# Three quarters of the up projection as pairs of panels, seven block products a pair

## The chip, the cores and the metric

One core of a Trainium2 chip. The time of a kernel is its device time in microseconds, the median of its runs. The engines are TensorE (PE; weight loads are listed apart as PEld), VectorE (DVE), ScalarE (ACT), GpSimd (POOL) and SyncE (SP, which here only issues DMAs).

## The reference

One layer of a decoder trunk in float32: 512 prompt tokens and 8 single-token samples share the weights. Both attentions end in `mix` and `h`; what the change touches is the feed-forward, whose product with `w_up` (1024 x 4096) is followed by a squared relu.

```python
mix = jax.nn.sigmoid(ga) * (oa @ w_pa) + jax.nn.sigmoid(gb) * (ob @ w_pb)
h = x + mix @ w_o
f = jnp.square(jax.nn.relu(rmsnorm(h, g_norm2) @ w_up))
return h + f @ w_down
# D_MODEL = 1024, D_FF = 4096; then y = rmsnorm(h + f @ w_down, g_final)
```

The outputs are also the caches moved on by a token, 42 MB of them plain copies from input to output.

## The kernel before

Activations lie transposed: 128 partitions, 8 tiles of the inner dimension (`k`), 520 columns (512 prompt and 8 sample tokens, in two halves `HC` of 260). A product of float32 is made in fp32r: weights and activations are each split into a high and a low part, and three matmuls are added up: high x high, high weight x low activation, low weight x high activation (`passes`). ScalarE makes the high part (`whi`, L86), VectorE the low one (`wlo`, L87), in pieces of 4 inner tiles (128x512).

The weights come in panels of 128 output columns, in the order of the list `order` in `run()`: the input projection, `w_pa`, `w_pb`, `w_o` (8 panels), then four quarters `qd` of the feed-forward, each of 8 panels of `w_up` and 8 of `w_down`; the last eight `w_down` panels (`lw`) run in column groups at the end (L1212). `panel_mms` loads panel i+2 on SP's queue, splits panel i+1, and issues the 48 matmuls of panel i (`k_tile`, L137), each 128x128 weights by 128x260. Four buffers hold split weights (`wbufs`).

After each `w_o` panel VectorE adds it to the residual `H`, and ScalarE and VectorE make `hh` and `hl`, the two parts of `H` times the norm's weight; the squares are summed in `acc`. Behind the first `w_up` panel two matmuls over `ones` (into `r2`) sum `acc` over the partitions; `rv` becomes the mean square and then its reciprocal (L1171). The feed-forward is homogeneous, so `rv` is first used in the last quarter. Each `w_up` panel is followed by ScalarE's relu from PSUM, VectorE's square and the two parts `fh` and `fl`; each `w_down` panel by an add into `dd` on VectorE. After each panel `pace()` puts one 1 MiB copy of a cache on POOL's DMA queue, which starts when the panel's last matmul is done, until the 42 copies are out.

A scheduler, fed with estimated durations, sets the order of the instructions on each engine; each engine then runs its own in that order. `tc.high_priority()` lets what is inside go ahead of what is ready, and `behind(x, y)` keeps two instructions in order.

Of the kernel before, what the change touches and what calls it, by code (L numbers as in the profile page):

```python
# [45 lines left out]
class Build:  # L46
    def __init__(self, ctx, tc, I, O):
# [32 lines left out]
    def raw_tile(self, i):  # L80
        return self.rawp.tile([P, self.panels[i][1], P], F32, tag="raw", name="raw", bufs=self.rawb)

    def split_piece(self, raw, x, n, dst=None):
        nc = self.nc
        hi, lo = dst or (self.wp.tile([P, n, P], F32R, tag=t, name=t, bufs=self.wbufs) for t in ("whi", "wlo"))
# [883 lines left out]

    def run(self):  # L970
# [146 lines left out]
        nc.vector.tensor_tensor(oal, self.oa, oah.bitcast(F32), op=ALU.subtract)  # L1117
        obh, obl = self.big("obh", F32R), self.big("obl", F32R)
        self.split_big(self.R, obh, obl)
        with pool("late") as p:  # L1120
            for x in range(2):
                for k, ps in enumerate(self.panel_mms(oah, oal, 4), 4 * x):
                    ga = halves(gA[:, k])
                    for o, i in ((ga[:, 0], ps[0]), (ga[:, 1], ps[1])) if isinstance(ps, list) else ((ga, ps),):
                        nc.vector.tensor_tensor(o, i, o, op=ALU.mult)
# [26 lines left out]
            self.rawp, self.rawb = p, 3  # L1152
            fh, fl = self.big("fh", F32R), self.big("fl", F32R)
            dd = self.big("dd")
            for qd in range(4):
# [4 lines left out]
                for k in range(KT):  # L1160
                    if qd == 3 and k == KT - 1:
# [3 lines left out]
                    if qd == 0 and k == 0:  # L1165
                        for j in range(2):
                            pr = self.bank("r2")
                            nc.tensor.matmul(pr[:, :HC], self.ones, acc[:, j * HC:(j + 1) * HC], start=True, stop=True)
                            nc.vector.tensor_scalar(rv[:, j * HC:(j + 1) * HC], pr[:, :HC], 1 / D, EPS,
                                                    op0=ALU.mult, op1=ALU.add)  # L1170
# [226 lines left out]
```

## Time and profile before

| | |
| --- | --- |
| median of 3 runs | 910.67 us (910.57 to 910.96) |
| span of the profiled execution, first to last instruction | 909.0 us |
| busy: PE, PEld | 898.3 (99%), 881.4 (97%) |
| busy: DVE, ACT, POOL | 548.6 (60%), 368.2 (41%), 72.3 (8%) |
| mean granted clock of TensorE | 0.996 |
| moved by DMA | 155.72 MB, mean 171 GB/s |

The profiled execution's own time is its span; the median of the runs, which hold no profile, lies 1.7 us above it. A group's row gives the source line, engine, operation, what is written and read, the shape and count; then the busy time and the mean of one in ns; then the idle time of that engine just before these instructions and what ended it. The chain of waits follows the instruction that ended last back to what released each step. A row of time stretches gives the busy time and count for each engine, the granted clock, the share of the DMA engines and GB/s.

### The profile page before, as it was taken

What the parts mean: (1) busy time and instruction counts of PE and PEld (TensorE: products, weight loads), DVE (VectorE), ACT (ScalarE), POOL (GpSimd) and SP (SyncE); (2) the same over time, 40 slices, a digit from 0 to 9 for tenths busy, and PEclk for the clock granted to TensorE, in tenths of its full rate; (3) what the DMA queues carried; (4) which work ended last, traced back from release to release, by engine and by line L of the source; (5) the groups of instructions that cost most, each with busy time, mean ns of one, the idle gap of its engine ahead of it and who ended that gap; (6) DMA issues with size and microseconds to landing.
All of it is one profiled execution on the core that took longest, in us unless ns stands there. A gap on an engine that the chain in (4) does not pass through costs nothing.

```text
span 909.0 us, 19543 instructions
## 1 busy us (share of the span) xinstructions
PE 898.3 (99%) x8154; PEld 881.4 (97%) x8154; DVE 548.6 (60%) x1083; ACT 368.2 (41%) x732; POOL 72.3 (8%) x127
## 2 busy tenths in 40 slices
PE   9999999999999999999999999999999999999996
PEld 8999999999999999999999999999999999999995
DVE  6867666865957769586655564433443345556643
ACT  6234324453645454456333444323432243224432
POOL 1110000000111212010000000000000000000000
PEclk9999999999999999999999999999999999999998
DMA  7476365324634632221688787777772222223302
GB/s 252 142 247 217 118 211 209 118 71 144 211 109 155 234 125 103 88 72 53 227 320 289 277 301 278 279 274 282 267 276 107 94 93 94 93 94 116 117 14 82
DMA packets 37728, 155.72 MB, mean 171 GB/s; under 512 B 5308, under 2 KB 10436, under 8 KB 35816
## 3 DMA queue, kind: packets, MB, share of 16 engines
q1 hardware_dynamic: 32248, 94.79, 29.8%
q0 software_dynamic: 5104, 59.20, 18.2%
q8 instruction: 64, 1.05, 0.5%
q10 hardware_dynamic: 288, 0.49, 0.1%
q14 instruction: 24, 0.20, 0.1%
HBM read 140.73 MB, written 54.17 MB: 214 GB/s over the span
## 4 chain that ended last, share of the span: by engine, by line
PE 98%; DMA 1%; DVE 0%; ACT 0%; SPq 0%; DVEq 0%; issue 0%; ACTq 0%
PE mps L137 83%; PE mps L1212 5%; PE mps L298 1%; PE lev L727 1%; PE sps L473 1%; PE pvp L506 1%; PE gpo L836 1%; PE gpu L840 1%; PE ptp L490 1%; PE vps L437 1%; PE gpo L838 1%; DMA xr<-in_xT 1%; PE gso L908 0%; PE gop L860 0%; PE gsp L925 0%; PE gps L668 0%
## 5 line engine op out<-in xcount | busy, mean ns | idle before, releaser
L86 ACT ACTIVATE whi<-raw 128x512 fp32r<-128x512 f32 (+1 forms) x266 | 165.0, 624 | 367.5 <-PE mps L137 339.0
L87 DVE TENSOR_TENSOR wlo<-raw,whi 128x512 fp32r<-128x512 f32 (+1 forms) x266 | 180.5, 681 | 130.0 <-ACT whi L86 128.8
L137 PE MATMUL mps<-uh,whi 128*128 128x260 f32 x896 | 255.9, 286 | 0.0
L137 PE MATMUL mps<-ul,whi 128*128 128x260 f32 x896 | 255.8, 286 | 0.0
L137 PE MATMUL mps<-uh,wlo 128*128 128x260 f32 x896 | 255.3, 285 | 0.0
L137 PEld LDWEIGHTS mps<-uh,wlo 128*128 128x128 f32 x896 | 168.8, 188 | 2.1 <-issue 1.5
L137 PEld LDWEIGHTS mps<-ul,whi 128*128 128x128 f32 x896 | 168.8, 188 | 1.2 <-issue 0.3
L137 PEld LDWEIGHTS mps<-uh,whi 128*128 128x128 f32 x896 | 168.8, 188 | 1.1 <-issue 0.7
L137 PE MATMUL mps<-hh,whi 128*128 128x260 f32 x512 | 144.8, 283 | 0.0
L137 PE MATMUL mps<-hh,wlo 128*128 128x260 f32 x512 | 144.8, 283 | 0.0
L137 PE MATMUL mps<-hl,whi 128*128 128x260 f32 x512 | 144.2, 282 | 0.0
L137 PE MATMUL mps<-fh,whi 128*128 128x260 f32 x384 | 108.2, 283 | 0.0
L137 PE MATMUL mps<-fh,wlo 128*128 128x260 f32 x384 | 108.1, 283 | 0.0
L137 PE MATMUL mps<-fl,whi 128*128 128x260 f32 x384 | 107.7, 282 | 0.0
L137 PEld LDWEIGHTS mps<-hh,whi 128*128 128x128 f32 x512 | 96.4, 188 | 0.0
L137 PEld LDWEIGHTS mps<-hh,wlo 128*128 128x128 f32 x512 | 96.3, 188 | 0.0
L137 PEld LDWEIGHTS mps<-hl,whi 128*128 128x128 f32 x512 | 96.3, 188 | 0.0
L137 PEld LDWEIGHTS mps<-fh,whi 128*128 128x128 f32 x384 | 72.3, 188 | 0.0
L137 PEld LDWEIGHTS mps<-fh,wlo 128*128 128x128 f32 x384 | 72.1, 188 | 0.0
L137 PEld LDWEIGHTS mps<-fl,whi 128*128 128x128 f32 x384 | 72.1, 188 | 0.0
L1212 PE MATMUL mps<-fh,lw 128*128 128x280 f32 (+1 forms) x256 | 46.8, 284 | 0.0
L1212 PEld LDWEIGHTS mps<-fh,lw 128*128 128x128 f32 x256 | 39.7, 189 | 0.1
(343 smaller groups left out, 1388.5 us busy)
## 6 DMA issues: line engine op xcount, KB each, us to landing
raw<-in_w_in SPq DMA_DIRECT2D x55, 512.0 KB, 4.3
raw<-in_w_up SPq DMA_DIRECT2D x32, 512.0 KB, 4.2
raw<-in_w_down SPq DMA_DIRECT2D x32, 512.0 KB, 4.3
sx<-in_state SPq DMA_DIRECT2D x8, 512.0 KB, 4.2
sx<-dV SPq DMA_DIRECT2D x8, 512.0 KB, 4.8
out_sgla<-sx POOLq DMA_DIRECT2D x8, 512.0 KB, 5.4
raw<-in_w_pb SPq DMA_DIRECT2D x8, 512.0 KB, 3.3
raw<-in_w_o SPq DMA_DIRECT2D x8, 512.0 KB, 7.1
```

What stands on the lines that cost most here:

```text
L86: self.piece = (nc.scalar.activation(hi, raw[:, x:x + n], AF.Copy), nc.vector.tensor_tensor(lo, raw[:, x:x + n], hi.bitcast(F32), op=ALU.s ...
L87: nc.vector.tensor_tensor(lo, raw[:, x:x + n], hi.bitcast(F32), op=ALU.subtract))
L137: self.last = self.nc.tensor.matmul(o[:, :HC], wt, x[:, k, j * HC:(j + 1) * HC], start=(k == 0 and n == 0), stop=(k == kt - 1 and n == 2))
L298: self.last = nc.tensor.matmul(ps[i][:, j, :HC], wt, u[:, k, j * HC:(j + 1) * HC], start=(k == 0 and n == 0), stop=(k == KT - 1 and n == 1))
L437: nc.tensor.transpose(pt[:, r * P:(r + 1) * P], vt[:, r * P:(r + 1) * P], self.c["ident"])
L473: m = nc.tensor.matmul(pss[hh][:, hp, c], Q[rows, i, b * P:(b + 1) * P], K[rows, i, ks], start=True, stop=True)
L490: nc.tensor.transpose(pt[:, hh, x], prs[hp][:, hh, x * P:(x + 1) * P], self.c["ident"])
L506: m = nc.tensor.matmul(po[64 * hh:64 * hh + 64, hp * P:(hp + 1) * P], v, pTs[hp][:, hh, x], start=(x == first), stop=(x == 1))
L727: m = self.nc.tensor.matmul(out, w, x, start=True, stop=True)
L836: nc.tensor.matmul(po[:, :256], ST[:, c], V[:, c], start=True, stop=(c == 0))
L838: nc.tensor.matmul(po[:, :256], qe[:, c * P:(c + 1) * P], st, start=False, stop=True)
L1212: nc.tensor.matmul(ps, w, u[:, kk, cc], start=(kk == 0 and x == 0), stop=(kk == KT - 1 and x == 2))
```

## The change

In quarters 0 to 2 (the prediction's quarters 1 to 3) two `w_up` panels are one entry of `order`, marked `PAIR`. Let the first panel's inner tiles 0 to 3 be A11 and 4 to 7 be A12, the second's A21 and A22, and B11, B12, B21, B22 the blocks of the activations (`hh`, `hl`), the first index the half of the inner tiles and the second the half of the columns. The second panel's results come out with the sign turned, so that its weights' sums need no subtraction. Each product is 4 inner tiles x 3 passes = 12 matmuls:

| product | weights | activations |
| --- | --- | --- |
| P1 | A11 | B11 |
| P5 | A21+A22 | B11-B12 |
| P2 | A12 | B21 |
| P6 | A11+A21+A22 (`s2`) | -(B11-B12+B22) |
| P3 | A11+A12+A21+A22 (`s4`) | B22 |
| P7 | A11+A21 | B22-B12 |
| P4 | A22 | B11-B12+B22-B21 |

PSUM adds P2 to P1, P3 to P5 and P7 to P6. The first panel's halves are P1+P2 and (P1+P6)+(P5+P3), the second's, with the sign turned, (P1+P6+P7)+P4 and (P1+P6+P7)+P5. VectorE's P1+P6 is the prediction's v6. P1 and P5 are copied from PSUM by ScalarE for these adds.

The weights' sums come in three ways: `sums` is loaded with the second panel (A21, A22), and a DMA of POOL's queue that adds to what is there (`accum_op=ALU.add`, 512 KB) turns it into A11+A21 and A21+A22; POOL makes `s2` and `s4` from it with two adds; `ra` (the first panel) and `rb` (A22) are plain loads. That is 7 split pieces a pair where two panels had 4. The sums of activations, T with the parts `Th` and `Tl`, are made tile by tile behind each `w_o` panel (`column_sums`) from a float32 copy `hg` of what `hh` and `hl` are split from. `AHEAD` is how many pieces the code splits ahead of the product in hand; `first_pairs` are the pairs that open a quarter: they run P2 before P6, the others P6 before P2. A fifth buffer of split weights and a third of raw panels lie in the pool `late`. Constants that the feed-forward does not use move to the pool `mid`, closed before it, and the feed-forward's work tiles share the name `t`. `pace()` is called once a pair instead of once a panel.

```diff
+    def load_pair(self, i):
+        ap, p = self.panels[i][0], self.late
+        sums = p.tile([P, KT, P], F32, tag="sums", name="sums", bufs=2)
+        self.load(sums, ap[1])
+        self.nc.gpsimd.dma_start(sums.rearrange("p (i k) n -> p i (k n)", i=2),
+                                 ap[:, :, :4].rearrange("i p k n -> p i (k n)"), accum_op=ALU.add)
+        ra = self.raw_tile(KT)
+        self.load(ra, ap[0])
+        rb = p.tile([P, 4, P], F32, tag="rb", name="rb", bufs=2)
+        self.load(rb, ap[1][:, 4:])
...
+    def pair_pieces(self, i):
...
+        yield self.split_piece(ra, 0, 4)
+        yield self.split_piece(sums, 4, 4)
+        s2, s4 = new(), new()
+        nc.gpsimd.tensor_tensor(s2, sums[:, 4:], ra[:, :4], op=ALU.add)
+        nc.gpsimd.tensor_tensor(s4, s2, ra[:, 4:], op=ALU.add)
...
+    def pair_mm(self, acts, done):
...
+        mid = (("P2", a, False), ("P6", b, True)) if i in self.first_pairs else (("P6", b, True), ("P2", a, False))
+        prev = None
+        for q, (n, o, fresh) in enumerate((("P1", a, True), ("P5", c, True), *mid, ("P3", c, False), ("P7", b, False),
+                                           ("P4", a, True))):
+            with self.tc.high_priority():
+                self.pieces_to(i, q + AHEAD)
+            if q == 4 and i + 2 < len(self.panels):
+                self.load_panel(i + 2)
+            hi, lo = self.ready[i][q]
+            for k in range(4):
+                xh, xl = acts(n, k)
+                for x, (w, u) in enumerate(((hi, xh), (hi, xl), (lo, xh))):
...
+                    if prev is not None:
+                        self.behind(mm, prev)
...
+    def column_sums(self, p, b, k, hi, lo):
...
+            e = nc.vector if k == KT - 1 else nc.gpsimd
+            e.tensor_tensor(t[:, 0], b22, b12, op=ALU.subtract)
+            nc.vector.scalar_tensor_tensor(t[:, 1], t[:, 0], -1.0, b11, op0=ALU.mult, op1=ALU.subtract)
+            nc.vector.scalar_tensor_tensor(t[:, 2], t[:, 1], -1.0, b21, op0=ALU.mult, op1=ALU.subtract)
...
+        nc.scalar.activation(hi[:, x, ts], t, AF.Copy)
+        nc.vector.tensor_tensor(lo[:, x, ts], t, hi[:, x, ts].bitcast(F32), op=ALU.subtract)
...
+    def up_pair(self, p, work, k, fh, fl):
...
+        def split(x):
+            nc.scalar.activation(t[x], t[x], AF.Square)
+            nc.scalar.activation(fh[:, k + x], t[x], AF.Copy)
+            nc.vector.tensor_tensor(fl[:, k + x], t[x], fh[:, k + x].bitcast(F32), op=ALU.subtract)
...
+            if n in ("P1", "P5"):
+                v[n] = new(n)
+                with tc.high_priority():
+                    nc.scalar.activation(v[n], o, AF.Copy)
+            elif n == "P2":
+                nc.scalar.activation(t[0][:, one], o, AF.Relu)
+            elif n == "P6":
+                v[n] = new(n)
+                with tc.high_priority():
+                    nc.vector.tensor_tensor(v[n], v["P1"], o, op=ALU.add)
+            elif n == "P3":
+                nc.vector.tensor_tensor(t[0][:, two], v["P6"], o, op=ALU.add)
+                nc.scalar.activation(t[0][:, two], t[0][:, two], AF.Relu)
+                split(0)
+            elif n == "P7":
+                v[n] = new(n)
+                nc.vector.tensor_tensor(v[n], v["P1"], o, op=ALU.add)
+                nc.vector.tensor_tensor(t[1][:, two], v[n], v["P5"], op=ALU.add)
+            else:
+                nc.vector.tensor_tensor(t[1][:, one], v["P7"], o, op=ALU.add)
+                nc.scalar.activation(t[1], t[1], AF.Relu, scale=-1.0)
+                split(1)
+                self.pace(1)
...
-            order += [(I["w_up"][qd * 8 + i], KT) for i in range(8)]
+            if qd < 3:
+                self.first_pairs.add(len(order))
+                order += [(I["w_up"][qd * 8 + i:qd * 8 + i + 2], PAIR) for i in range(0, 8, 2)]
...
+                nc.scalar.activation(hg[:, k], H[:, k], AF.Copy, scale=self.g("n2", k))
+                nc.vector.tensor_tensor(hl[:, k], hg[:, k], hh[:, k].bitcast(F32), op=ALU.subtract)
+                self.column_sums(p, hg, k, Th, Tl)
...
+                if qd < 3:
+                    for k in range(0, KT, 2):
+                        self.pair_mm(acts, self.up_pair(p, work, k, fh, fl))
+                        if qd == 0 and k == 0:
+                            spread()
```

What this does to the order shows at three places. On VectorE, where the first `w_up` panel ends and the reciprocal stands, before (`L87` is a low part of weights, `L1178` and `L1180` the first panels' square and low part):

```order
L1169 TENSOR_SCALAR rv<-r_7061 128x260
L87 TENSOR_TENSOR wlo<-raw,whi 128x512
L1169 TENSOR_SCALAR rv<-r_7064 128x260
L1178 SCALAR_TENSOR_TENSOR fsq<-mps,relu 128x520
L1171 RECIPROCAL rv<-rv 128x520
L1180 TENSOR_TENSOR fl<-fsq,fh 128x520
L87 TENSOR_TENSOR wlo<-raw,whi 128x512 x2
L1178 SCALAR_TENSOR_TENSOR fsq<-mps,relu 128x520
```

And the same place of the changed kernel (`L1072` is the last of the last tile's three T sums, `L1075` T's low part, `L108` a low part of weights, `L1098` v6, `L1100` the add for P3):

```order
L1072 SCALAR_TENSOR_TENSOR tr<-tr,hg 128x260
L1318 TENSOR_SCALAR rv<-r_7224 128x260
L108 TENSOR_TENSOR wlo<-raw,whi 128x512
L1318 TENSOR_SCALAR rv<-r_7227 128x260
L1075 TENSOR_TENSOR Tl<-tr,Th 128x780
L1320 RECIPROCAL rv<-rv 128x520
L1098 TENSOR_TENSOR P_7149<-P_7096,mps 128x260
L108 TENSOR_TENSOR wlo<-sums,whi 128x512
L108 TENSOR_TENSOR wlo<-s,whi 128x512
L108 TENSOR_TENSOR wlo<-raw,whi 128x512
L1100 TENSOR_TENSOR t<-P_7149,mps 128x260
```

The reciprocal stood behind the first panel's square; it now stands between T's low part and v6.

On TensorE, where the first panel of quarter 2 ends and the second begins, before:

```order
L137 MATMUL mps_8035<-hh_6469,whi_7970 128x260
L137 MATMUL mps_8035<-hl_6470,whi_7970 128x260
L137 MATMUL mps_8035<-hh_6469,wlo_7971 128x260
L137 MATMUL mps_8101<-hh_6469,whi_8027 128x260
L137 MATMUL mps_8101<-hl_6470,whi_8027 128x260
L137 MATMUL mps_8101<-hh_6469,wlo_8028 128x260
```

And the changed kernel where P2 of quarter 2's first pair ends (its PSUM tile is `mps_8165`, the next pair's `mps_8313`):

```order
L189 MATMUL mps_8165<-hh_6474,whi_8108 128x260
L189 MATMUL mps_8165<-hl_6475,whi_8108 128x260
L189 MATMUL mps_8165<-hh_6474,wlo_8109 128x260
L189 MATMUL mps_8313<-hh_6474,whi_8238 128x260
L189 MATMUL mps_8313<-hl_6475,whi_8238 128x260
L189 MATMUL mps_8165<-Th_6477,whi_8167 128x260
L189 MATMUL mps_8165<-Tl_6478,whi_8167 128x260
L189 MATMUL mps_8165<-Th_6477,wlo_8168 128x260
```

Where one panel followed another whole, two matmuls of the next pair's P1 now stand between this pair's P2 and its P6. Inside a quarter the queue goes on in this manner, two pairs in turn: the next pair's P1, this pair's P7, the next one's P5 and P6, this one's P4, the next one's P2 and P3.

On POOL, the copies from the first `w_pb` panel to the last copy, before:

```order
L179 DMA out_ca1k<-in_ca1k 16x16384
L179 DMA out_ca1v<-in_ca1v 16x16384
L179 DMA out_ca2k<-in_ca2k 16x16384 x4
L179 DMA out_ca2v<-in_ca2v 16x16384 x4
L179 DMA out_ca3k<-in_ca3k 16x16384 x16
L179 DMA out_ca3v<-in_ca3v 16x16384 x16
```

And a stretch of quarter 1 in the changed kernel (`L96` is the adding DMA, `L124` and `L125` make `s2` and `s4`, `L267` is a cache copy):

```order
L96 DMA sums<-in_w_up 128x2x512
L124 TENSOR_TENSOR s<-sums,raw 128x512
L125 TENSOR_TENSOR s<-s,raw 128x512
L267 DMA out_ca3k<-in_ca3k 16x16384
L96 DMA sums<-in_w_up 128x2x512
L124 TENSOR_TENSOR s<-sums,raw 128x512
L267 DMA out_ca3k<-in_ca3k 16x16384
L125 TENSOR_TENSOR s<-s,raw 128x512
L267 DMA out_ca3k<-in_ca3k 16x16384 x6
```

POOL's queue held nothing but copies in this stretch; adding DMAs and adds now stand in it between them, in order.

More of the change, by code (lines that the diff above doesn't have):

```diff
@@ L29 @@
 LEVELS = (64, 32, 16, 8, 4, 2)
+PAIR = "pair"
+AHEAD = 4
 def pv(t):
@@ L78, in load_panel, with raw_tile @@
         self.loaded = m
[L80 to L81 removed]
+    def raw_tile(self, kt):
+        self.nraw += 1
+        pool, bufs = (self.late, 1) if self.late is not None and self.nraw % 3 == 0 else (self.wp, 2)
+        return pool.tile([P, kt, P], F32, tag="raw", name="raw", bufs=bufs)
+    def load_pair(self, i):
[8 more added lines that the diff above has]
+        self.load(rb, ap[1][:, 4:])
+        self.raw[i] = (ra, rb, sums)
     def split_piece(self, raw, x, n, dst=None):
         nc = self.nc
[L85 removed]
+        hi, lo = dst or self.weight_tiles(n)
         self.piece = (nc.scalar.activation(hi, raw[:, x:x + n], AF.Copy),
@@ L88, in split_piece, with weight_tiles, pieces_to @@
         return hi, lo
+    def weight_tiles(self, n):
+        self.nw += 1
+        pool, bufs = (self.late, 1) if self.late is not None and self.nw % 5 == 0 else (self.wp, self.wbufs)
+        return [pool.tile([P, n, P], F32R, tag=t, name=t, bufs=bufs) for t in ("whi", "wlo")]
+    def pair_pieces(self, i):
+        nc = self.nc
+        ra, rb, sums = self.raw.pop(i)
+        new = lambda: self.late.tile([P, 4, P], F32, tag="s", name="s", bufs=3)
+        yield self.split_piece(ra, 0, 4)
[3 more added lines that the diff above has]
+        nc.gpsimd.tensor_tensor(s4, s2, ra[:, 4:], op=ALU.add)
+        order = {"12": lambda: self.split_piece(ra, 4, 4), "s2": lambda: self.split_piece(s2, 0, 4),
+                 "s4": lambda: self.split_piece(s4, 0, 4), "s3": lambda: self.split_piece(sums, 0, 4),
+                 "22": lambda: self.split_piece(rb, 0, 4)}
+        for n in (("12", "s2") if i in self.first_pairs else ("s2", "12")) + ("s4", "s3", "22"):
+            yield order[n]()
+    def pieces_to(self, i, n):
+        if i >= len(self.panels):
+            return
+        if self.panels[i][1] != PAIR:
+            if n > 0 and i not in self.split:
+                self.split_panel(i)
+            return
+        if i not in self.jobs:
+            self.jobs[i], self.ready[i] = self.pair_pieces(i), []
+        while len(self.ready[i]) < min(n, 7):
+            self.ready[i].append(next(self.jobs[i]))
+        if n > 7:
+            self.pieces_to(i + 1, n - 7)
     def split_panel(self, i):
+        if i in self.split:
+            return
+        if self.panels[i][1] == PAIR:
+            return self.pieces_to(i, AHEAD - 1)
         src, kt = self.panels[i]
@@ L228, in start @@
         self.c = {"gcols": gc}
-        raw = [self.raw_tile(i) for i in range(2)]
+        raw = [self.raw_tile(KT) for i in range(2)]
         x = [xr[:, i] for i in (6, 0, 1, 2, 3, 4, 5, 7)]
@@ L974, in run @@
         order = []
+        self.first_pairs = set()
         ix = self.pidx
@@ L1164, in run @@
                     ps = self.panel_mm(hh, hl)
[L1165 to L1170, printed above, removed]
-                        nc.vector.reciprocal(rv, rv)
-                    t = p.tile([P, NT], F32, tag="relu", name="relu", bufs=2)
-                    if qd == 3:
-                        nc.vector.scalar_tensor_tensor(halves(t), ps, 0.0, halves(rv), op0=ALU.max, op1=ALU.mult)
-                    else:
-                        nc.scalar.activation(halves(t), ps, AF.Relu)
-                    f = p.tile([P, NT], F32, tag="fsq", name="fsq", bufs=2)
+                    t = work()
+                    nc.vector.scalar_tensor_tensor(halves(t), ps, 0.0, halves(rv), op0=ALU.max, op1=ALU.mult)
+                    f = work()
                     nc.vector.scalar_tensor_tensor(halves(f), ps, 0.0, halves(t), op0=ALU.max, op1=ALU.mult)
```

87 lines of the change are left out of this document (67 added, 20 removed).

## The prediction

> **What bounds the kernel now.** First the page's busy times and its chain of waits by engine, then the chain in order of time, then two stretches of the feed-forward as windows: quarter 1's up projection and its down projection.
>
> ```profile
> span 909.0 us, 19543 instructions
> PE 898.3 (99%) x8154; PEld 881.4 (97%) x8154; DVE 548.6 (60%) x1083; ACT 368.2 (41%) x732; POOL 72.3 (8%) x127
> ...
> PE 98%; DMA 1%; DVE 0%; ACT 0%; SPq 0%; DVEq 0%; issue 0%; ACTq 0%
> ...
> 535.42 0.88 PE r L1168 x4
> 536.30 315.77 PE mps L137 x2640
> ...
> core 0: us, PE busy (x) PEld busy (x) DVE busy (x) ACT busy (x) POOL busy (x), PEclk, DMA share, GB/s
> 536.30:582.20 45.90, 45.90 (x386) 45.90 (x386) 24.90 (x35) 18.26 (x31) 3.41 (x7) 1.00 0.75 274
> 582.20:628.20 46.00, 46.00 (x387) 46.00 (x386) 15.93 (x24) 10.23 (x17) 3.89 (x8) 1.00 0.76 275
> ```
>
> TensorE ends 98% of the chain; from 536.30 on, 2640 matmuls follow each other without a hole, at full clock: 315.77/2640 = 119.6 ns each. A panel of 48 lasts 5.74 us. VectorE works 24.90 of an up quarter's 45.90 us and ScalarE 18.26. Only fewer matmuls, or a hole, can move the end.
>
> **The change, part by part.** Removed: a pair of panels takes 7 x 12 = 84 matmuls instead of 96, all of the same 128x260 form. Twelve pairs drop 144: 144 x 119.6 ns = **-17.2 us**. A pair lasts 84 x 119.6 = 10.05 us, a product of 12 lasts 1.435 us.
>
> What the other engines pay per pair comes from rows of the same shape, or the nearest:
>
> ```profile
> L87 DVE TENSOR_TENSOR wlo<-raw,whi 128x512 fp32r<-128x512 f32 x258 | 177.5, 689 | 130.0 <-ACT whi L86 128.8 <-ACT Va L492 0.6
> L1180 DVE TENSOR_TENSOR fl<-fsq,fh 128x520 fp32r<-128x520 f32 x32 | 22.4, 699 | 22.2 <-ACT fh L1179 22.1
> L1125 DVE TENSOR_TENSOR gA<-mps,gA 128x260 f32<-128x260 f32 x8 | 3.1, 428 | 1.2 <-PE mps L137 1.2
> L1171 DVE RECIPROCAL rv<-rv 128x520 f32<-128x520 f32 x1 | 3.4, 3393 | 0.0
> L86 ACT ACTIVATE whi<-raw 128x512 fp32r<-128x512 f32 x258 | 162.1, 630 | 366.8 <-PE mps L137 339.0 <-DMA raw<-in_w_in 15.4 <-issue 4.2
> L1179 ACT ACTIVATE fh<-fsq 128x520 fp32r<-128x520 f32 x32 | 20.4, 637 | 29.9 <-DVE fsq L1178 29.9
> L1176 ACT ACTIVATE relu<-mps 128x520 f32<-128x520 f32 x24 | 14.1, 588 | 0.0
> L1141 ACT ACTIVATE hh<-H,gcols 128x520 fp32r<-128x520 f32 x8 | 5.9, 732 | 1.3 <-DVE H L1140 1.3
> L787 ACT ACTIVATE D<-D 128x256 f32<-128x256 f32 x24 | 9.9, 414 | 9.6 <-DVE D L785 9.6
> L849 ACT ACTIVATE jk<-gpo 128x256 f32<-128x256 f32 x16 | 6.0, 377 | 0.0
> ```
>
> VectorE: 7 low parts of weights x 0.689, 5 adds of half width x 0.428, 2 low parts of results x 0.699 = 8.36 us. ScalarE: 7 x 0.630, 4 of half width x 0.377, then a full-width relu, two squares and two copies at 0.59 to 0.64 (3.1) = 9.0 us. Both fit under 10.05, with little air. Five weight buffers let a piece be split up to four products ahead, so these run beside TensorE unless one comes late.
>
> Start of quarter 1. Between the last `w_o` panel and the first P7, VectorE has 13 instructions of sums and splits in its queue after H, then the reciprocal, and only then the add v6 = P1+P6, for which P7 waits. How fast a reader follows a matmul:
>
> ```profile
> 529.40 0.28 PE L137 MATMUL mps<-mh,wlo 128*128 128x260 f32 x1
> ...
> 529.72 0.70 DVE L1140 TENSOR_TENSOR H<-mps,H 128x520 f32<-128x520 f32 x1 [1.58 <-PE mps L137]
> ```
>
> That is 0.32 us after the last matmul's start, 0.20 after its slot ends. With the end of `w_o` as zero: H is done at 0.9, hh at 1.7, hg at 2.3 (0.732 each). TensorE runs P1 and P5 to 2.87 and P2 to 4.31, which wants hh's last tile at 3.95: in time. Then come the two sums over `ones`, to about 5.1 (0.88 in the chain above), two matmuls of the next P1, and P6. VectorE meanwhile has hl, the three T sums of the last tile (0.428 each, each waiting for the one before) and splits between them: the last T sum at 5.85. T's high half (780 columns; 0.414 at 256 and 0.630 at 512 make that 0.86, an estimate) stands in ScalarE's queue behind the relu of P2, and is ready near 6.85; P6's last step wants it at 6.4: 0.45 lost. VectorE ends T's low half (about 1.0) at 8.0, the reciprocal at 11.3, v6 at 11.6. TensorE has P3 and two matmuls as cover and wants v6 at 10.1: 1.5 lost. Sum **+2.0** (ends: 0, if VectorE runs ahead of this count; 3.4, the whole reciprocal). Before, a full panel stood behind the reciprocal and hid it.
>
> Start of quarters 2 and 3. After P2, TensorE's queue has two matmuls of the next pair's P1, whose weights take the buffer that P2's last use frees, and then P6, which waits for the relu of P2. ScalarE does that split first (0.20 + 0.63) and then the relu: P6 begins 1.05 late, with 0.24 of matmuls inside: **+0.8** each, 1.6 together (ends: 0 and 1.2 each). In quarter 1 the `ones` matmuls cover this.
>
> The other nine pairs. The shortest cover is P4's 1.435 between P6 and P2, in which VectorE must read P6 (0.20 + 0.428); up to two splits of 0.69 stand ahead in its queue, and POOL's two adds a pair can stop it. POOL's only two-input add and VectorE beside it:
>
> ```profile
> 344.77 3.88 POOL L752 TENSOR_TENSOR qe<-qe,QKb 128x512 f32<-128x512 f32 x1 [6.32 <-DVE el L751]
> ...
> 345.12 0.69 DVE L757 TENSOR_TENSOR kl<-kl,QKb 128x512 f32<-128x512 f32 x1
> 345.72 0.42 DVE L770 TENSOR_TENSOR qx<-D,QKb 128x256 f32<-128x256 f32 x1
> ...
> 347.40 0.70 DVE L966 TENSOR_TENSOR gA<-mps,rb 128x520 f32<-128x520 f32 x1
> 348.01 0.92 DVE L789 TENSOR_TENSOR D<-D,QKb 128x256 f32<-128x256 f32 x1
> 348.85 0.41 DVE L790 TENSOR_TENSOR D<-D,QKb 128x256 f32<-128x256 f32 x1
> ...
> 389.88 1.60 POOL L752 TENSOR_TENSOR qe<-qe,QKb 128x512 f32<-128x512 f32 x1 [12.32 <-DVE el L751]
> ```
>
> The add that begins at 344.77 ends at 348.65, 1.25 us after VectorE took an operand from PSUM at 347.40; the next VectorE instruction with two SBUF inputs takes 0.92 instead of 0.42. So I charge 0.5 of VectorE per POOL add: 8.36 + 1.0 = 9.4 of 10.05. Successive starts lie 0.60 apart where one lasts 0.69, so the true load is lower. It fits on the average; for late v6's I take 0.25 a pair, **+2.3** (ends: 0, and 0.85 a pair, 7.7). The Trainium skill, "SBUF — State Buffer", section "SBUF: two separate sides", calls that port pair "an exclusive lock", held for the whole instruction; the trace agrees (0.92 for 0.42), but shows the lock taken late, once VectorE leaves the port.
>
> Transfers. A pair moves 1.75 MiB instead of 1.0 on top of the paced cache copies.
>
> ```profile
> raw<-in_w_up SPq DMA_DIRECT2D x32, 512.0 KB, 4.2
> out_sgla<-sx POOLq DMA_DIRECT2D x8, 512.0 KB, 5.4
> kcb<-in_vc POOLq DMA_DIRECT2D x3, 1024.0 KB, 6.0
> out_ca3v<-in_ca3v POOLq DMA_DIRECT2D x16, 5.3
> L752 POOL TENSOR_TENSOR qe<-qe,QKb 128x512 f32<-128x512 f32 x4 | 10.1, 2520 | 59.3 <-DVE el L751 59.3
> ```
>
> Per pair, 1.75 MiB and one 1 MiB copy in 10.05 us are 287 GB/s against the 274 that took 0.75 of the DMA engines: the bytes are hidden. The time A of the adding DMA from issue to landing has no row: between 4.2 us (a plain load) and 10.8 (twice the 5.4 of a store of that size). I take 6.0, POOL's own load of 1 MiB, since an add also reads what it adds to. It counts through POOL's queue. In a quarter, pair 3's sums go out once pair 1 has split its own (about 3 to 4.6) and land 4.2 later, at 9 (quarter 1) or 7.4; then A, two POOL adds (2.52 each), in quarters 1 and 3 a cache copy (about 4 of its 5.3 before the next transfer begins), and only then pair 4's adding DMA, again A. Quarter 1: 18.5 + 2A, wanted at 30.2 (242 matmuls and the holes above, less its split); quarter 3: 16.7 + 2A, wanted at 28.3; quarter 2, without the copy, 12.7 + 2A. At 6.0 they lose 0.3, 0.4 and 0: **+0.7** (ends: 0 up to 5.8; 9.9 + 10.0 + 6.0 = 25.9 at 10.8). SP's queue holds no other engine's work; its loads only wait for buffers.
>
> `w_o` panels. The sums of activations add to each panel on VectorE at most two adds of 0.428 and a low part of 780 columns (about 1.0): with splits, H, hl and acc about 5.3 of 5.74, on ScalarE about 4.2. TensorE reads none of it before quarter 1: 0, bounded by 1. Memory moves and the pools' renamed buffers issue nothing: 0. The tail's code is the same: 0.
>
> Sum: -17.2 + 2.0 + 1.6 + 2.3 + 0.7 = -10.6. The profiled execution spans 909.0, 1.7 under the 910.67 median, which I keep as what lies around it: 898.4 + 1.7 = **900.1 us**.
>
> **Rivals.** (a) Late sums. At A = 8 the last pairs of the three quarters lose 4.3 + 4.4 + 0.4 = 9.1 instead of 0.7: 908.5. At 10.8 it is 25.9: 925, slower than before; the point between is A = 8.6. For it: two adding DMAs in a row with POOL's adds between, all in order. Against: no row of this size took over 5.4. The Trainium skill, "Collectives: The Full Stack", section "The bandwidth ceiling: the fold count and why AG ≠ RS ≠ AR", says that an adding transfer reads two sources and so moves at half the rate of a copy. By that, 10.8 and 925 would be what to expect; no run here shows it yet, and 6.0 already counts the second read as bytes, with the fixed part of a transfer counted once.
>
> (b) Slower: VectorE becomes the bound. If each POOL add shuts it out for its shortest whole length, 1.60 us, a pair needs 8.36 + 3.2 = 11.6 us, 1.5 over TensorE's; 12 x 1.5 = 18.0, more than the saving: 910.7 - 17.2 + 18.0 + 3.6 (the starts) = 915. It decides above 17.2/12 = 1.43 a pair, so at 1.55 us per POOL add; the trace has 0.5.
>
> (c) No gain: TensorE's queue alternates two pairs in a fixed order, and each wait in it stops both. Waits of 1.43 a pair give 910.7. The order leaves at least 0.7 us at each step that I walked.
>
> **How the numbers follow.** Forecast 0.78, own range 895.5 (2 us of waits in all) to 904.5 (A = 7); (a) 0.12, half of it below 908.8, 0.02 within 0.2%, 0.04 slower; (b) 0.07; (c) 0.03. The range 895 to 908 leaves out (b), (c) and half of (a). The runs before lie within 0.04% of each other; 0.2%, 1.8 us, is what I call a change. Faster 0.84, same 0.05, slower 0.11.
>
> **What would show it.** Matmul count 144 lower, 119.6 ns apart inside the pairs; a hole of some 1.5 us before quarter 1's first P7 released by v6, and 0.8 before P6 of quarters 2 and 3 released by ScalarE; VectorE near 0.8 busy in the pair stretches. Wrong if TensorE there waits for the adding DMA's splits (a), or VectorE is above 0.95 busy and releases TensorE in every pair (b).

## The result, and the profile after

The changed kernel takes 915.07 us (median of 5 runs, 912.75 to 915.88) where the kernel before takes 910.76: a ratio of 1.0042 with a 95% interval of 1.0029 to 1.0054. It is slower, by about 4 us, where 10.6 us less were forecast; 915.07 lies above the range of 895 to 908. Its profiled execution, 913.32 us with a span of 911.5, is one of the faster ones.

The page's head and TensorE's waits (what waited, for whom; us in total, times, the longest). `L189` is a pair's matmul, `L225` a single panel's, `L107` and `L108` the two parts of weights, `L1092` a copy of P1 or P5, `L1098` v6, `L1108` the add that reads P4, `L1298` H:

```profile
span 911.5 us, 19609 instructions
PE 888.3 (97%) x8010; PEld 868.0 (95%) x8010; DVE 596.2 (65%) x1172; ACT 417.7 (46%) x844; POOL 128.9 (14%) x170
...
PE mps L189 <- ACT P L1092: 6.1, 1, 6.1
PE mps L189 <- DVE wlo L108: 2.3, 2, 1.5
PE mps L225 <- DVE t L1108: 1.6, 3, 0.5
PE mps L189 <- ACT whi L107: 1.5, 3, 0.6
...
PE mps L189 <- DVE H L1298: 1.0, 1, 1.0
PE mps L189 <- DVE P L1098: 0.8, 3, 0.3
```

The 144 matmuls are gone (8010 for 8154), but TensorE, which had no holes in the feed-forward, now waits. Quarter by quarter, up and down projection together, from the end of `w_o`, first before and then after:

```profile
529.40:622.15 92.75, 92.75 (x775) 92.63 (x773) 42.60 (x61) 30.54 (x50) 7.78 (x16) 1.00 0.74 267
622.15:714.01 91.86, 91.86 (x771) 91.86 (x769) 37.49 (x56) 29.29 (x48) 5.35 (x11) 1.00 0.60 220
714.01:805.87 91.86, 91.86 (x771) 91.86 (x770) 46.59 (x70) 29.29 (x48) 0.00 (x0) 1.00 0.26 92
```

```profile
528.96:628.10 99.14, 90.97 (x726) 89.39 (x725) 63.38 (x99) 49.66 (x91) 25.44 (x28) 0.97 0.76 255
628.10:716.32 88.22, 87.02 (x722) 86.41 (x721) 50.16 (x80) 43.01 (x80) 22.55 (x25) 1.00 0.81 275
716.32:808.56 92.24, 88.17 (x723) 86.71 (x722) 58.49 (x94) 42.98 (x80) 10.01 (x10) 1.00 0.44 144
```

A quarter of 720 matmuls at 119.6 ns would last 86.1 us, quarter 1 with its sums over `ones` 87.0. So quarter 1 loses 12.1 us, quarter 2 2.1, quarter 3 6.1: 20.3 lost against 17.2 saved.

Where they are lost, from the distances between the starts of TensorE's instructions beyond 119.6 ns: quarter 1's start 10.5 us; the late sums of quarter 3 4.0; the starts of quarters 2 and 3 together 1.7; the ends of the three up projections 3.4 (1.1 each: the second down panel waits 0.52 for the read of P4, L1108, and short waits follow); the rest 0.7.

**Quarter 1's start**, in the timeline of TensorE (the bracket: idle time and what ended it), and the clock around it:

```profile
533.08 0.28 PE L189 MATMUL mps<-Th,wlo 128*128 128x260 f32 x1
539.46 0.58 PE L189 MATMUL mps<-hh,whi 128*128 128x260 f32 x1 [6.09 <-ACT P L1092]
539.84 0.42 PE L189 MATMUL mps<-hl,whi 128*128 128x260 f32 x1
```

```profile
533.40:539.40 6.00, 0.00 (x0) 0.00 (x0) 5.45 (x10) 3.92 (x8) 1.94 (x3) 0.86 0.49 176
539.40:544.40 5.00, 4.95 (x19) 4.54 (x20) 3.32 (x8) 2.44 (x6) 0.00 (x0) 0.50 0.60 208
544.40:549.40 5.00, 4.73 (x38) 4.52 (x38) 5.00 (x5) 2.06 (x4) 1.27 (x1) 0.98 0.75 148
```

P2 adds onto P1 in PSUM, so ScalarE must first have copied P1 (L1092); the copy stands in ScalarE's queue behind the last `w_o` tiles' work and comes 6.1 us late. Then TensorE's granted clock is 0.50 for 5 us, and matmuls start 0.217 us apart: 2.0 us more. The `w_o` work is late because of POOL and VectorE:

```profile
509.03 1.29 POOL L96 DMA_DIRECT2D sums<-in_w_up  x1 [5.08 <-DMA sums<-in_w_up]
...
516.20 1.43 POOL L124 TENSOR_TENSOR s<-sums,raw 128x512 f32<-128x512 f32 x1 [4.56 <-DMA sums<-in_w_up]
...
520.28 1.29 POOL L1070 TENSOR_TENSOR tr<-hg 128x260 f32<-128x260 f32 x1
...
525.30 1.25 POOL L1070 TENSOR_TENSOR tr<-hg 128x260 f32<-128x260 f32 x1 [3.26 <-ACT hg L1300]
527.74 1.47 POOL L124 TENSOR_TENSOR s<-sums,raw 128x512 f32<-128x512 f32 x1 [1.19 <-DMA sums<-in_w_up]
```

```profile
521.61 0.43 DVE L1071 SCALAR_TENSOR_TENSOR tr<-tr,hg 128x260 f32<-128x260 f32 x1 [5.12 <-POOL tr L1070]
...
522.42 0.69 DVE L1298 TENSOR_TENSOR H<-mps,H 128x520 f32<-128x520 f32 x1
...
525.86 1.25 DVE L1308 TENSOR_TENSOR acc<-acc,t 128x520 f32<-128x520 f32 x1
...
527.97 1.52 DVE L1072 SCALAR_TENSOR_TENSOR tr<-tr,hg 128x260 f32<-128x260 f32 x1
529.41 0.69 DVE L1298 TENSOR_TENSOR H<-mps,H 128x520 f32<-128x520 f32 x1
...
535.31 0.69 DVE L1298 TENSOR_TENSOR H<-mps,H 128x520 f32<-128x520 f32 x1
```

The first pairs' adding DMA and the adds that wait for it stand in POOL's queue between the differences of T (L1070). VectorE's next sum waits 5.12 us for one of them, and behind that sum stands H of the next panel. H comes at 522.42, 529.41 and 535.31, 5.9 to 7.0 us apart where TensorE needs 5.74 for a panel. VectorE does not catch up, since its instructions beside POOL's are stretched (`acc` at 525.86 from 0.69 to 1.25 beside L1070, the T sum at 527.97 from 0.43 to 1.52 beside L124).

**Quarter 3's late sums**, on POOL:

```profile
733.22 0.56 POOL L267 DMA_DIRECT2D out_ca3v<-in_ca3v  x1
735.98 1.22 POOL L96 DMA_DIRECT2D sums<-in_w_up  x1 [2.21 <-DMA sums<-in_w_up]
...
747.37 1.27 POOL L124 TENSOR_TENSOR s<-sums,raw 128x512 f32<-128x512 f32 x1 [4.58 <-DMA sums<-in_w_up]
```

The last pair's adding DMA goes out 19.5 us into the quarter (17.1 in quarter 2), behind a cache copy, and takes 11.3 us. Its plain load had stood on SP until 732.20, for the split of A11+A21 two pairs before, which frees the tile.

### The profile page after: what moved, and what is told of

Same layout as the page of the kernel before. It is cut to its first block, busy times and chain, and to the rows that moved or that the text cites. A ratio compares the mean times of both kernels' runs of the same rounds, so it can differ in the third digit from the quotient of the medians.

```text
span 911.5 us, 19609 instructions
## 1 busy us (share of the span) xinstructions
PE 888.3 (97%) x8010; PEld 868.0 (95%) x8010; DVE 596.2 (65%) x1172; ACT 417.7 (46%) x844; POOL 128.9 (14%) x170
## 5 line engine op out<-in xcount | busy, mean ns | idle before, releaser
L107 ACT ACTIVATE whi<-raw 128x512 fp32r<-128x512 f32 (+1 forms) x242 | 149.3, 621 | 288.7 <-PE mps L225 237.6
L225 PE MATMUL mps<-uh,whi 128*128 128x260 f32 x896 | 255.8, 286 | 0.0
L225 PE MATMUL mps<-ul,whi 128*128 128x260 f32 x896 | 255.7, 285 | 0.0
L225 PE MATMUL mps<-uh,wlo 128*128 128x260 f32 x896 | 255.2, 285 | 0.0
L108 DVE TENSOR_TENSOR wlo<-raw,whi 128x512 fp32r<-128x512 f32 (+1 forms) x242 | 165.8, 689 | 70.2 <-ACT whi L107 68.4
L225 PEld LDWEIGHTS mps<-uh,wlo 128*128 128x128 f32 x896 | 168.7, 188 | 2.1 <-issue 1.5
L225 PEld LDWEIGHTS mps<-ul,whi 128*128 128x128 f32 x896 | 168.7, 188 | 1.2 <-issue 0.3
L225 PEld LDWEIGHTS mps<-uh,whi 128*128 128x128 f32 x896 | 168.7, 188 | 1.1 <-issue 0.7
L225 PE MATMUL mps<-fh,whi 128*128 128x260 f32 x384 | 108.6, 284 | 1.8 <-DVE t L1108 1.6
L225 PE MATMUL mps<-fh,wlo 128*128 128x260 f32 x384 | 108.4, 283 | 0.0
L225 PE MATMUL mps<-fl,whi 128*128 128x260 f32 x384 | 108.1, 282 | 0.0
L225 PEld LDWEIGHTS mps<-fh,whi 128*128 128x128 f32 x384 | 72.0, 188 | 3.0 <-DVE t L1108 2.2
L225 PEld LDWEIGHTS mps<-fh,wlo 128*128 128x128 f32 x384 | 72.3, 188 | 0.0
L225 PEld LDWEIGHTS mps<-fl,whi 128*128 128x128 f32 x384 | 72.2, 188 | 0.0
L189 PE MATMUL mps<-Th,wlo 128*128 128x260 f32 x192 | 53.4, 283 | 2.3 <-DVE wlo L108 2.3
L189 PE MATMUL mps<-Th,whi 128*128 128x260 f32 x192 | 54.4, 285 | 0.5 <-DVE P L1098 0.3
L189 PE MATMUL mps<-Tl,whi 128*128 128x260 f32 x192 | 53.9, 282 | 0.0
L189 PE MATMUL mps<-hh,whi 128*128 128x260 f32 x144 | 42.3, 294 | 8.8 <-ACT P L1092 6.1
L189 PE MATMUL mps<-hl,whi 128*128 128x260 f32 x144 | 41.3, 287 | 0.0
L189 PE MATMUL mps<-hh,wlo 128*128 128x260 f32 x144 | 40.7, 286 | 0.0
```

The costliest lines, as they stand in the source:

```text
L107: self.piece = (nc.scalar.activation(hi, raw[:, x:x + n], AF.Copy), nc.vector.tensor_tensor(lo, raw[:, x:x + n], hi.bitcast(F32), op=ALU.s ...
L108: nc.vector.tensor_tensor(lo, raw[:, x:x + n], hi.bitcast(F32), op=ALU.subtract))
L189: mm = nc.tensor.matmul(o, w[:, k], u, start=(fresh and k == 0 and x == 0), stop=(k == 3 and x == 2), skip_group_check=True)
L225: self.last = self.nc.tensor.matmul(o[:, :HC], wt, x[:, k, j * HC:(j + 1) * HC], start=(k == 0 and n == 0), stop=(k == kt - 1 and n == 2))
```

## The experiments

Times and ratios of each are against runs of the kernel before on the same chip (910.4 to 911.0).

**e1.** T's differences on VectorE.

```diff
-            nc.gpsimd.tensor_tensor(t[:, 0], b11, b12, op=ALU.subtract)
+            nc.vector.tensor_tensor(t[:, 0], b11, b12, op=ALU.subtract)
-            e = nc.vector if k == KT - 1 else nc.gpsimd
+            e = nc.vector
```

> All first differences of the T sums (seven tiles) go from POOL to VectorE; nothing else changes. Theory 1 (POOL's queue: the difference of a w_o tile stands behind POOL's add s2, which waits for the adding DMA, so VectorE's sums and its next H come 5 us late, and the w_o epilogues run into quarter 1): VectorE's wait of 5.1 us for tr is gone, TensorE's hole of 6.1 us before quarter 1's P2 shrinks to about 1 us (P1's copy still stands behind the last w_o tile's work on ScalarE), the 0.22 us matmul spacing after it is gone, and the time falls by 6 to 10 us to 905 to 909. Rival 2 (VectorE simply has more than the 5.74 us of a w_o panel to do): 0.42 us more per panel makes the lag larger, the hole is 6 us or more, and the time is 914 to 918.

911.49 (908.71 to 915.38), ratio 1.0014 (0.9996 to 1.0031). The wait for P1's copy fell from 6.1 to 1.1 us in the profiled run:

```profile
PE mps L189 <- DVE P L1098: 2.1, 2, 1.4
...
PE mps L189 <- ACT P L1092: 1.1, 1, 1.1
```

Rival 2 falls: more work on VectorE made it better. Theory 1's hole shrank as it said, but the time missed its 905 to 909; only 3.6 us came of it. TensorE now waits 1.4 for v6 behind the reciprocal, and quarter 3 lost 8 us instead of 6: the granted clock fell to 0.57 there for 6 us, after waits of a size that left it at 1.00 in the changed kernel. The runs spread over 6.7 us. The edit also takes seven instructions off POOL, so it does not by itself separate the wait in POOL's queue from POOL's cost to VectorE; e3 and h2 do.

**e2.** The adding DMA without its addition.

```diff
-                                 ap[:, :, :4].rearrange("i p k n -> p i (k n)"), accum_op=ALU.add)
+                                 ap[:, :, :4].rearrange("i p k n -> p i (k n)"))
```

> The adding DMA becomes a plain one of the same 512 KB into the same place; the addition A11+A21, A21+A22 is left out. Theory 1 with a dear addition: the landing time falls from a median of 8.6 us to about 4.5, POOL's queue is stopped for a shorter time in w_o and quarter 3's sums come in time: 4 to 8 us faster, 907 to 911. Rival 3 (the transfer is slow because it stands behind 1 MiB cache copies and shares the DMA engines, not because it adds): the median stays above 7.5 us and the time within 1.5 us of 914.

914.01 (910.46 to 916.15), ratio 1.0026 (1.0012 to 1.0040). The landing rows, of the changed kernel and of e2:

```profile
sums<-in_w_up POOLq DMA_DIRECT2D x12, 512.0 KB, 8.6
```

```profile
sums<-in_w_up POOLq DMA_DIRECT2D x12, 512.0 KB, 7.4
```

The addition costs 1.2 us of 8.6; the shortest one took 4.1 instead of 5.7. Theory 1's 4.5 is missed: the addition is the smaller part of what makes the transfer slow, and the hole of 6.1 us stayed.

**e3.** All four sums of a pair by POOL from plain loads.

```diff
-        self.nc.gpsimd.dma_start(sums..., ap..., accum_op=ALU.add)
-        self.load(rb, ap[1][:, 4:])
+        nc.gpsimd.tensor_tensor(s1, sums[:, 4:], sums[:, :4], op=ALU.add)
+        nc.gpsimd.tensor_tensor(s2, s1, ra[:, :4], op=ALU.add)
+        nc.gpsimd.tensor_tensor(s4, s2, ra[:, 4:], op=ALU.add)
+        nc.gpsimd.tensor_tensor(s3, sums[:, :4], ra[:, :4], op=ALU.add)
```

> No adding DMA and no separate load of A22: both panels of a pair are loaded as they are, and POOL makes all four sums with four adds a pair instead of two. Theory 1: POOL's queue no longer waits long for transfers, so the w_o lag and its hole shrink to about 1 us and quarter 3's late sums are gone: 901 to 906. Rival 4 (POOL's adds shut VectorE out of its operands): four adds a pair cost VectorE 2 us more of its 10 us, holes of 0.5 us or more before the products appear in every pair, and the time is 908 to 914.

918.41 (917.82 to 919.76), ratio 1.0082 (1.0067 to 1.0097). The late sums are nearly gone; v6 takes their place (`L1096` here, `L1090` the copy of P1):

```profile
PE 889.6 (97%) x8010; PEld 868.7 (95%) x8010; DVE 615.7 (67%) x1172; ACT 417.7 (46%) x844; POOL 149.6 (16%) x182
...
PE mps L187 <- DVE P L1096: 8.6, 7, 2.9
PE mps L187 <- ACT P L1090: 4.6, 1, 4.6
```

VectorE has the same 1172 instructions and is busy 19.5 us longer for 24 more POOL adds: 0.81 us each. Rival 4 has the direction right, but the time lies outside its 908 to 914, and v6 is late at seven places, not in every pair. The hole fell to 4.6 only. From 484 to 545 us VectorE waits for none of T's differences here; it is its instructions beside POOL's four adds that are stretched (the sum `acc`, `L1306`, and a low part of weights, `L104`, take 0.69 and 0.68 undisturbed), and that is enough to keep `w_o`'s work behind:

```profile
509.38 1.79 DVE L1306 TENSOR_TENSOR acc<-acc,t 128x520 f32<-128x520 f32 x1
511.09 1.86 DVE L104 TENSOR_TENSOR wlo<-raw,whi 128x512 fp32r<-128x512 f32 x1
```

**e4.** No cache copy after a pair (`self.pace(1)` removed from `up_pair`).

> The one cache copy after each pair is left to later places (the pairs issue none; the copies not yet out at the end of the third quarter are issued there). Theory 1: quarter 1's start keeps its hole of about 6 us, and only quarter 3's late sums (some 3.5 us of holes in its last pairs, where the adding DMA took 11.3 us behind a copy) go: 1.5 to 4 us faster, 910 to 913. Rival 3 (contention with copies is what delays everything, w_o too): more than 6 us faster, below 908.

914.63 (913.93 to 916.00), ratio 1.0041 (1.0026 to 1.0056): above theory 1's 913 and far above rival 3's 908. The hole stayed at 6.1, a panel of `w_o` waited 2.9 for H, quarter 3's late sums cost about half, and the median landing was 8.2. This does not clear the copies. The edit removes only those behind pairs; behind `w_o` and down panels six adding DMAs still ran beside one, those of `w_o` among them, so rival 3 is not tested there. The three that lost their copy landed sooner: 10.7 became 6.6, 8.4 became 7.4, 11.3 became 8.3. The changed kernel's own trace agrees: its three adding DMAs with no cache copy under way landed in 5.7 each, its nine beside one in 7.1 to 11.3. The stretches of the last two of quarter 3, from issue to landing, without a copy and with one (share of the DMA engines and GB/s at the end; a packet counts where it begins):

```profile
724.47:730.20 5.73, 5.73 (x49) 5.73 (x49) 4.54 (x9) 4.34 (x9) 1.27 (x1) 1.00 0.67 130
735.98:747.30 11.32, 11.32 (x97) 11.32 (x96) 6.15 (x12) 6.21 (x12) 1.74 (x2) 1.00 1.07 351
```

So the time beyond 5.7 goes with what else moves. How much of it is copies and how much the pair's own loads stays open: in g1 one took 10.1 beside loads alone.

**f1.** e1, with the sums over `ones` and the reciprocal behind quarter 1's third down panel.

```diff
-                        if qd == 0 and k == 0:
-                            spread()
...
+                    if qd == 0 and k == 2:
+                        spread()
```

> As e1 (T's differences on VectorE), and the two sums over ones with the reciprocal move from behind quarter 1's first pair into its down projection. If the prediction's step is right (the reciprocal's 3.4 us ahead of v6 makes TensorE wait 1.5 us; e1's trace has 1.5), that wait goes and the time falls by 1 to 2 us against e1 (911.5), to about 910. Rival: T's low part and the splits are late at the same place, so nothing is won (911 to 912).

915.17 (914.25 to 917.53), ratio 1.0053 (1.0036 to 1.0070): a miss. The scheduler issued the reciprocal earlier than it was written, among quarter 1's last pair, ahead of v7 = P1+P6+P7:

```profile
571.40 3.40 DVE L1320 RECIPROCAL rv<-rv 128x520 f32<-128x520 f32 x1
...
575.27 0.41 DVE L1105 TENSOR_TENSOR P<-P,mps 128x260 f32<-128x260 f32 x1
```

P4 waited 3.3 us for it. Also, P1's copy was 3.6 late where e1's profile had 1.1, with the same code in `w_o`: VectorE's T sums there took 1.52 and 1.75 us beside POOL's adds. Whether that is the spread of e1's runs, two profiles cannot show.

**g1.** P6 and P7 in a PSUM tile of their own, the last P4 of a quarter too; the reciprocal as in f1.

```diff
-        m, c = self.pm.tile([P, 2, 512], F32, tag="m", name="mps"), self.bank("mps")
-        a, b = m[:, 0, :HC], m[:, 1, :HC]
+        m, c, b = self.pm.tile([P, 2, 512], F32, tag="m", name="mps"), self.bank("mps"), self.bank("mps")
+        a, d = m[:, 0, :HC], (self.bank("mps") if last else m[:, 1])[:, :HC]
```

> Off the changed kernel: P6 and P7 get a PSUM tile of their own instead of the second bank of P1's and P2's tile, a quarter's last P4 goes to a bank of its own, and the reciprocal moves as in f1; T's differences stay on POOL. Theory 5 (TensorE waits for reads of the other bank of the same tile: P6 for the relu of P2, and the second down panel for the read of P4): the waits of 0.76 and 0.1 us at the start of quarters 2 and 3 and of 0.68, 0.1, 0.24 and 0.1 at the end of all three are gone, 5 us in sum, 909 to 911; the hole of 6.1 us stays. Rival: each wait is replaced by the next one (the split of the weights, the next tile's buffer), and less than 2 us is won (912.5 or more).

912.99 (907.99 to 917.61), ratio 1.0022 (0.9998 to 1.0047). The waits at the starts and ends of the quarters are gone; what is left at the end of quarter 1, 0.4, is the two sums over `ones`. But the time is not theory 5's 909 to 911, and the rival fits: other waits took their place. P4, which now has the second bank of P2's tile, waits up to 5.1 us for the relu of P2, which stands on ScalarE behind a split that waits for the sums: late sums by another way.

**g2** is g1 and e1 together.

> g1 and e1 together. If the causes add up (theories 1 and 5): 911.5 less 1.5 (v6) less 4.5 (banks) = 905 to 906, with quarter 3's late sums (some 5 us in e1) still there. If they don't, 908 or more.

906.81 (903.07 to 908.10), ratio 0.9949 (0.9928 to 0.9970): less than 1 us above what the causes add up to. Quarter 3 still loses 5.8 us.

**g3.** g2, and `sums` as two tiles.

```diff
+        self.load(s1, ap[1][:, 4:])
+        self.nc.gpsimd.dma_start(s1, ap[1][:, :4], accum_op=ALU.add)
...
+        self.load(s3, ap[1][:, :4])
+        self.nc.gpsimd.dma_start(s3, ap[0][:, :4], accum_op=ALU.add)
```

> g2, and the tile of the sums is split in two, A21+A22 and A11+A21, each with its own load and its own adding DMA of 256 KB, so that the first need not wait until the second one's last reader is done. Theory 6 (quarter 3's last pair waits because the load of its sums stands on SP behind the split of A11+A21 two pairs before): the late sums vanish, 3 to 5 us less than g2, 900 to 903. Rival 3 (the transfers themselves are slow): within 1.5 us of g2.

901.08 (899.18 to 905.24), ratio 0.9902 (0.9869 to 0.9934). As theory 6 said, quarter 3's late sums are gone. Only quarter 1's start still waits (`L110` is a low part of weights, `L1095` the copy of P1):

```profile
PE mps L192 <- DVE wlo L110: 2.4, 1, 2.4
PE mps L192 <- ACT P L1095: 2.2, 1, 2.2
```

**h3.** The two tiles alone, on the changed kernel.

> Off the changed kernel, only the split of the sums' tile into two with an adding DMA each. Theory 6: quarter 3's late sums (3.7 us of holes) go, quarter 1's 12 us stay: 910 to 912. Rival: in w_o one adding DMA more stands in POOL's queue ahead of T's differences, the hole at quarter 1 grows, and the time is 914 to 918.

915.19 (915.02 to 915.22), ratio 1.0045 (1.0030 to 1.0060): theory 6 missed the time, and the rival's 914 to 918 holds it. Quarter 3 no longer waits for sums, but the hole is 6.1, a `w_o` panel waits 1.7 for H, and v6 costs 2.8 in four waits (0.8 in the changed kernel).

**h4.** g3 with `s2` and `s4` on VectorE.

```diff
-        nc.gpsimd.tensor_tensor(s2, s1, ra[:, :4], op=ALU.add)
-        nc.gpsimd.tensor_tensor(s4, s2, ra[:, 4:], op=ALU.add)
+        nc.vector.tensor_tensor(s2, s1, ra[:, :4], op=ALU.add)
+        nc.vector.tensor_tensor(s4, s2, ra[:, 4:], op=ALU.add)
```

> As g3, with s2 and s4 added on VectorE instead of POOL. VectorE's own price is two more instructions of 0.69 us a pair. If a POOL add costs VectorE 0.8 us (VectorE's busy time grew by 19.5 us for 24 more POOL adds in e3), this is no loss: 898 to 902. If it costs the 0.5 us of the prediction or less, VectorE's load grows by some 0.4 us a pair and the pairs show holes: 902 to 907.

924.46 (917.55 to 925.01), ratio 1.0124 (1.0083 to 1.0165): outside both. VectorE's load did not grow (602.0 us busy in g3, 599.3 here with 24 instructions of 0.69 more, so 24 POOL adds had cost it 19.3), but the add (`L126`) now waits for the adding DMA in VectorE's queue, and a low part of weights (`L110`) and `hl` (`L1304`) come late behind it:

```profile
L126 DVE TENSOR_TENSOR s<-s,raw 128x512 f32<-128x512 f32 x4 | 2.8, 689 | 10.8 <-DMA s<-in_w_up 10.8
...
PE mps L192 <- DVE wlo L110: 9.8, 2, 5.8
PE mps L192 <- DVE hl L1304: 8.8, 1, 8.8
```

It is the changed kernel's fault with the queues exchanged: what waits for the transfer stops all that stands behind it.

**h2.** Only quarters 2 and 3 in pairs.

> Off the changed kernel: quarter 1 is single panels as before, quarters 2 and 3 stay in pairs; the sums T are made behind w_o as in the changed kernel. Theory 1 (the changed kernel loses 12 us in quarter 1, of which the pairs themselves are worth 5.7): the lag behind w_o is hidden by single panels, 6 us faster than the changed kernel, 906 to 909. Rival 2 (the work behind w_o holds up TensorE whatever follows): 912 or more.

906.83 (906.15 to 907.09), ratio 0.9953 (0.9938 to 0.9968), as theory 1 said: quarter 1 loses nothing here, quarters 2 and 3 keep 11.5 us of matmuls less 7.4 of waits. T's differences are still on POOL, but with no sums of weights to be made during `w_o` there is no lag: VectorE waits for TensorE ahead of each of the eight H, as in the kernel before.

**k1.** The first two panels of quarter 1 single, on the changed kernel.

```diff
+                    for k in range(2) if qd == 0 else ():
+                        ps = self.panel_mm(hh, hl)
+                        if k == 0:
+                            spread()
+                        ...
-                    for k in range(0, KT, 2):
+                    for k in range(0 if qd else 2, KT, 2):
```

> Off the changed kernel, one edit: the first two panels of quarter 1 are single panels again (the reciprocal behind the first of them, as in the kernel before); T's differences stay on POOL and the sums in one tile. Theory 1 (the 12 us of quarter 1 arise because pairs begin while the work behind w_o is late): 12 us of loss become at most 2, for 1.4 us of matmuls: 904 to 907. If it is instead the pairs of quarter 1 themselves (POOL's adds, late sums), the loss moves to its next pair: 910 or more.

909.31 (908.34 to 910.98), ratio 0.9979 (0.9966 to 0.9991), between the two. Quarter 1 loses 7.8 us instead of 12.1; single panels themselves now wait 2.8 us for hh, and the granted clock behind that is 0.66 for 5 us. The lag is large enough to stop any panel, while the sums for the next pairs are made beside `w_o`.

**h1.** g3 with these two single panels.

> As g3, and the first two panels of quarter 1 are single panels again (24 products' worth of matmuls more than a pair: 12 matmuls, 1.4 us). Theory 1: VectorE and ScalarE are behind after w_o, and plain panels need no T and no copy of P1, so the 5.0 us of holes at quarter 1's start in g3 go for 1.4 us of matmuls: 3 to 4 us faster than g3 (901.1), 897 to 898.5. Rival: the holes move to the first pair after them, and the time is 901 to 903.

897.18 (896.38 to 897.58), ratio 0.9847 (0.9832 to 0.9862): the fastest here, 13.7 us below the kernel before. TensorE waits for nobody between 500 and 800 us:

```profile
PE 884.0 (99%) x8022; PEld 866.2 (97%) x8022; DVE 602.8 (67%) x1173; ACT 413.0 (46%) x836; POOL 120.7 (13%) x171
```

132 matmuls fewer are 15.8 us; 13.7 of them arrive.

**k2.** The changed kernel once more.

> The changed kernel once more, for a second profile of it: its five runs lie between 912.75 and 915.88. If the spread comes from waits for transfers, the hole at quarter 1's start stays within 1 us of 6.1 and the waits for the sums of quarters 1 and 3 differ by some us; if it comes from the lag behind w_o, the hole itself differs.

913.21. The hole is 5.6, the late sums of quarter 3 again about 4 us; both profiles of this kernel are near its fast end, so what its slowest runs add stays open.

## Why the prediction was wrong

- *Removed matmuls, -17.2.* Right: 144 fewer, 119.6 ns each.
- *"`w_o` panels": "TensorE reads none of it before quarter 1: 0, bounded by 1".* This step failed. It counted VectorE's work per panel (5.3 of 5.74) and left out whom VectorE waits for: POOL's T differences, in one queue with an adding DMA and adds that wait for it. It also took no price there for POOL beside VectorE, which the prediction charged only inside the pairs. e1 (6.1 to 1.1 us of wait) and h2 (no sums of weights beside `w_o`, no lag) show the first; e3 shows the second, a copy 4.6 us late with no wait for POOL in VectorE's queue.
- *"Start of quarter 1", +2.0, ends 0 and 3.4.* It measured 10.5: 1.2 before P1, 6.3 before P2, 2.0 of slow clock, 1.0 for v6. The order of v6 behind the reciprocal was read rightly, and e1, where the hole is small, shows the two waits that make up the 2.0: 0.5 for T's high part and 1.5 for v6. But the walk began with VectorE and ScalarE on time, and it let P2 start without P1's copy, though P2 adds onto P1's place in PSUM.
- *"Start of quarters 2 and 3", +1.6.* It measured 1.7. The mechanism is right as well: TensorE waits for the split of the next P1's weights, and P6 begins 1.1 us after P2's last slot (1.05 was forecast). In g1, where P6 need not wait for P2's relu and follows P2 at once, the wait is gone.
- *"The other nine pairs", +2.3.* Quarter 1 lost 0.4 to v6 there, quarter 2 nothing. The price of a POOL add was too low: 0.8 us of VectorE (e3 and h4), not 0.5. It cost little: only four of quarter 2's eight adds ran within its pairs, and VectorE was busy 31.25 of their 40.20 us (first row below), 0.78 where near 0.8 was forecast. e3 and h3 show v6 late when something is added. Rival (b) needed 1.55 and did not decide; that its price, 915, is the measured time is chance.
- *"Late adding DMA", +0.7.* It measured 4.0, all in quarter 3. Taking A as 6.0 fits a transfer with no cache copy under way (5.7); the median was 8.6, and the one that came late took 11.3. "No row of this size took over 5.4" overlooked a load of the kernel before (second row below, 7.1). The working also took the last pair's load as issued in time, and it stood on SP for a tile; with two tiles (g3, h3) the late sums are gone. Rival (a)'s chain of transfers in one queue is this, at a third of the 12.7 that its terms give for A = 8.6: POOL's adds took 1.3 to 1.8 us, not 2.52, and no sums were late in quarters 1 and 2. (By the same terms the gain ends at A = 8.4, not 8.6, and A = 7 gives 904.1, not 904.5.) That a copy holds up the next transfer for about 4 us, no run shows; in the changed kernel a copy and an adding DMA went out 0.5 us apart (518.95 and 519.48), and the second landed in 8.2. The Trainium skill, "Collectives: The Full Stack", section "The bandwidth ceiling: the fold count and why AG ≠ RS ≠ AR", has a ring's ReduceScatter, whose adds read two sources, at half the rate of AllGather's copies, and calls that model ring-specific. This DMA's landing shows less: 8.6 against 7.4 us in the median, 5.7 against 4.1 at the least, a factor of 1.2 to 1.4.
- *Not in the sum:* 3.4 us at the quarters' ends, where the second down panel needs the PSUM tile that P4 is still read from (in g1, with P4 in a bank of its own, the wait is gone).

The stretch of quarter 2's pairs (VectorE's is the third busy time), and the loads of `w_o` before the change:

```profile
628.10:668.30 40.20, 39.60 (x330) 39.39 (x329) 31.25 (x51) 29.75 (x59) 10.73 (x11) 1.00 0.74 237
```

```profile
raw<-in_w_o SPq DMA_DIRECT2D x8, 512.0 KB, 7.1
```

The saving itself was real: h1, another kernel, with these waits mended and 12 matmuls more, stands at 897.2. What failed is the sum of waits, 6.6 in the forecast and 20.3 in the trace, nearly half of it (9.5) from the lag behind `w_o`.

## What to carry to other kernels

When a change gives a helper engine work that waits for transfers, go through that engine's queue in order and ask what else stands there, and who waits for that, also in the stage before the one that is changed. An engine with over 5 us of work in a panel of 5.74 does not catch up a lag, so a stage with no slack should not be handed work while the one before it is late; two panels of the old kind between them cost 1.4 us of matmuls and saved 5 of waits (g3 to h1, 3.9 net). Give what is read at different times its own tile: a shared one makes its users wait for each other.

## What the runs showed of the hardware

- After 6.1 us without a matmul TensorE was granted half its clock for 5 us (0.50, matmuls 0.217 us apart instead of 0.120). The Trainium skill, "TensorE: Matmul & The Clock Gate", section "Part 1: The HAM clock gate (the "warmup" mystery)", says that the gate opens after about 3.4 us of sustained work; here it took 4.9, with the short waits at the sums over `ones` in between. One long hole is not needed: in e1 the clock fell as well, to 0.57 for 6 us, after waits of 0.8 and 0.7 us that began 1.2 us apart.
- A POOL add of 128x512 (1.36 to 1.51 us in the mean of a line in e3) cost VectorE 0.8 us of busy time, by two experiments that change 24 of them, one each way.
- The adding transfer of 512 KB into SBUF landed in 5.7 us with no cache copy under way and in 7.1 to 11.3 beside one; without its addition it landed only 1.2 us sooner in the median.
